# A hybrid HGRN2, pooling and gated MLP trunk: a new column pitch for the Strassen quarters, another order around the mixer's seam, and deferred sums in the down projection

## The chip, the core and the metric

The kernel runs on one core of one Trainium2 chip. The metric is the device time of one execution in microseconds, as the median of several runs. Profiles are of one execution, taken by the hardware profiler. The engines are TensorE (PE in the profile; its weight loads are PEld), VectorE (DVE), ScalarE (ACT), GpSimd (POOL) and SyncE (SP, which issues most of the DMAs).

## The reference

One layer over 16 meta tokens and 1024 tokens of width 1024, all in fp32:

```python
u = rmsnorm(h, mix_norm_pre)                     # h: meta tokens, then x
q, f_logit, i_in, g_out, v_pool, gate_a, gate_b = split(u @ w_in)
a = hgrn2(q, f_logit, i_in, g_out, lbs, hgrn_out_norm)     # chunked recurrence, 4 heads
p = multiscale_pool(v_pool, pool_proj, pool_scale)         # windows 2, 4, 8, 16
z = sigmoid(gate_a) * (a @ w_branch_hgrn) + sigmoid(gate_b) * (p @ w_branch_pool)
h = h + rmsnorm(z @ w_out, mix_norm_post)
u = rmsnorm(h, ffn_norm_pre)
gt = causal_dwconv(u @ ffn_w_gate, ffn_conv_w, ffn_conv_b) # 3 taps along the tokens
y = (gelu_tanh(gt) * (u @ ffn_w_up)) @ ffn_w_down          # inner width 2816
h = h + rmsnorm(y, ffn_norm_post)                          # meta tokens dropped
```

## The kernel before, in words

**fp32 by three matmuls.** Each operand is split into a rounded part (`h`, `hi`) and the rest (`l`, `lo`), and a product is the sum of hi by hi, hi by lo and lo by hi, accumulated in PSUM. ACT makes the rounded part by a cast, DVE (at places POOL) the rest by a subtraction. `wsplit2` (L159 and L160) does this for the weights of the branch projections, `keep` (L917 and L918) for weights of the feed-forward that are prepared early and stored in DRAM (`kept...`), `wo_split` (L1201) for the output projection, `cut` (L1494 and L1495) for the down projection.

**Strassen.** The gates of the mixer and the gate and up projections of the feed-forward run in units by Winograd's form of Strassen's scheme: the weights and the activations are cut into quarters, and a unit has seven products P1, P2, P6, P5, P3, P7, P4 in this order, whose moving operands are the quarters b11, b21 and b22 and the sums t1 to t4 (P1: b11, P2: b21, P6: t2, P5: t1, P3: b22, P7: t3, P4: t4). A quarter has four blocks of 128 rows (one column of a tile each, `k`) with the tokens along the free axis. The causal convolution needs two tokens of halo ahead of the first half of the tokens, so b11, b21, t2 and t4 have 514 columns: two of halo, then 512. A gate unit uses all 514, in two cuts of 258 and 256 columns, for P1, P2, P6 and P4; an up unit needs no halo and reads 512 columns from column 2 on. P5, P3 and P7 are 512 columns without a halo. In `product` (L299, L300 and L302) a block of 512 columns is three matmuls, a block with a halo six of half the size. In the mixer's gates b11, b21 and b22 are columns of the normed tokens themselves (`uhi` and `ulo`, rows of 1088 columns); in the feed-forward they are cut from one large tile, b11 and b21 from `v1` (rows of 544 columns, 514 used) and b22 and t1 from `v2` (rows of 512). t2 and t4 are made by `two_halves` in slots of their own (rows of 514), t1 of the mixer and t3 too (rows of 512). A row is 4 bytes per column.

**Order by hand.** Between the gates and the end of the mixer the string `ORDER` sets which work comes after which: F, Q, G and PV are input projections, h steps of the heads, BB and BA the eight column blocks of the two branch projections (pool and hgrn), `sa` splits of the heads' outputs, and w0 to w5 steps that prepare the feed-forward's weights (`keep_first` and `keep_unit`). The branch weights come in pairs that share one raw load, one cast and one subtraction: (BB6, BA2), then (BB7, BA3), (BA4, BA5), (BA6, BA7). They are asked for a few jobs ahead.

**The mixer's output projection** runs in three chunks c of 2, 3 and 3 tiles of 128 tokens (`TILES`), each with eight steps over the inner blocks; the last two steps run tile by tile. A tile's sums stand in a pair of PSUM banks (`pm`); there are four pairs. `Row` holds what follows, in steps that the table `SEAM` sets among the steps of the next chunk: `take` reads the pair twice (DVE: `m`, L1332; ACT: the square, `junk`, L1333), `add` scales it and adds the residual row, `square` and `norm` are the norm ahead of the feed-forward, `feat` transposes the row on PE into the quarters. A number is the tile, m the meta rows, W splits the next weights.

**Down projection.** It too is cut by Strassen-like sums, in three groups `s_` of 11 steps k, each with two sets of four banks, `pa` and `pb`, and 24 matmuls a step (L183 to L185); `prep` casts the operands for two steps ahead into two turns of one tile `rot`. At the end of a group the banks are joined into SBUF sums c11, c12, c21, c22 and u2 (`acc`). After group 1, u2 = pb - c11, c21 = pa - u2 and c12 = c12 - u2. DVE does the first two from PSUM (L1694, L1695), POOL the last (L1696). The order of the instructions of this part on each engine is found by the compiler's scheduler, unlike that of the mixer, which is as written.

Of the kernel before, what the change touches and what calls it, by code (L numbers as in the profile page):

```python
# [9 lines left out]
F32R = mybir.dt.float32r  # L10
U8 = mybir.dt.uint8
AF = mybir.ActivationFunctionType
ALU = mybir.AluOpType
# [7 lines left out]
HALO = 2  # L21
# [7 lines left out]
SEAM = (("W", "W", "W", "W", "W", "W", "0.take 0.add", "W 0.square 1.take m.join 0.norm 1.add 1.square 1.norm"),  # L29
# [14 lines left out]
HT = 514  # L44
HN = HT - HALO
EARLY = 4
# [11 lines left out]
         "w4 sa2 BB3 w5 h3 BB4 w5 BB5 w5 sa0 sa3 BA0 w5 BA1 w2 BB6 w3 BA2 BB7 BA3 BA4 BA5 BA6 BA7")  # L58
# [10 lines left out]
def trunk_kernel(ctx: ExitStack, tc: tile.TileContext, x, meta_tokens, mix_norm_pre,  # L69
# [897 lines left out]
    def two_halves(dst, q):  # L967
        n = HN if q in ("t1", "t3") else HT
        for h in "hl":
            dst[q + h] = [slot(2 * n, F32R, q + h).rearrange("p (k t) -> p k t", k=2) for _ in range(2)]  # L970
# [159 lines left out]
    gens, after = {}, {}  # L1130
# [43 lines left out]
    for n, name, names in ((HT, "v1", ("b11h", "b11l", "b21h", "b21l")), (HN, "v2", ("b22h", "b22l", "t1h", "t1l"))):  # L1174
        v = ubig(F32R, name)
        v1 = v if n == HT else v1
        t = v.rearrange("p (i k t) -> p i k t", i=4, k=4)
        for i, q in enumerate(names):
            fq[q] = [t[:, i, :, :n] if n == HT else t[:, i, :, :].rearrange("p k t -> p (k t)")[:, : 4 * n].rearrange("p (k t) -> p k t", k=4)]
# [70 lines left out]
    def to_quarters(un, t_at, n, pt, eng):  # L1250
# [6 lines left out]
        if t_at < HT:  # L1257
            src = pt.rearrange("p (j k t) -> p j k t", j=2, k=4) if n == P else pt.rearrange("p j (k t) -> p j k t", k=4)
            hi, lo = (v1.rearrange("p (j h k t) -> p h j k t", j=2, h=2, k=4)[:, h, :, :, t_at : t_at + n] for h in range(2))
            act.copy(hi, src)  # L1260
            dve.tensor_tensor(lo, src, rr(hi), ALU.subtract)
            return {}
# [258 lines left out]
    def step(c, at, after=None):  # L1521
        w = wo.next()
        for i in TILES[c]:
            mix_tile(c, at, w, R[i].x, i - TILES[c][0])
            if after:
                after(i)
        if c == 0:
            mix_meta(at, w, R["m"].x)
        wo.ahead()
        next_z(1)  # L1530
# [17 lines left out]
    with tc.manual_schedule(engines={E.PE, E.Activation, E.DVE, E.Pool}):  # L1548
        for i in (1, "m", 0):
            R[i] = Row(0 if i == "m" else HALO + i * P, HALO if i == "m" else P, pair("pm"))  # L1550
        for c in range(3):
            for at in range(KD - LAST):
                step(c, at)
                run(*SEAM[c][at].split())
# [116 lines left out]
    for s_ in range(3):  # L1671
        banks = [[bank("pd") for _ in range(NT)] for _ in range(2)]
        for k in range(KH):
            at = s_ * KH + k
            for b_, o_ in zip(banks, preps.pop(at)):
                multiply(b_, o_, k == 0, k == KH - 1)
            ahead(at + 2)
            if at >= 3 and early and at % 3 == 0:
                load_ops(3, early[0][0])
            if at >= 3 and early and at % 3 == 1:  # L1680
                prep_last(*early.pop(0))
            if s_ == 2 and k in (KH - 6, KH - 4):
                for t in ((0, 1) if k == KH - 6 else (2, 3)):
                    load_h(NT + t)
            if s_ == 2 and k == KH - 3:
                load_ops(3, KH - 2)
                load_ops(3, KH - 1)
        pa, pb = banks
        for t in range(NT):
# [3 lines left out]
            elif s_ == 1:  # L1693
                dve.tensor_tensor(u2[t], pb[t], c11[t], ALU.subtract)  # L1694
                dve.tensor_tensor(c21[t], pa[t], u2[t], ALU.subtract)  # L1695
                pool_e.tensor_tensor(c12[t], c12[t], u2[t], ALU.subtract)  # L1696
# [55 lines left out]
```

## Time and profile before

| what | value |
|---|---|
| median of 3 runs | 1349.35 us (1348.93 to 1350.22) |
| the profiled execution, its own time | 1351.27 us |
| its span in the profile | 1349.6 us |
| mean granted TensorE clock | 0.995 |
| 500 to 575 us | branch projections BB, BA: PE busy 74.33 of 75.00 us |
| 575 to 700 us | mixer's output projection: PE busy 124.22 of 125.00 us |
| 700 to 1120 us | feed-forward gate and up: PE busy 419.99 of 420.00 us |
| 1120 to 1290 us | its end and the down projection: PE busy 167.45 of 170.00 us |

A profile row names the engine, the line and the operation, what it writes and reads, shapes and counts. Times are microseconds unless marked ns. A timeline row begins with the start and the duration; in square brackets stand the idle time of the engine before it and what released it. A PE matmul's duration includes its way through the array: the next one starts before it ends. A row of the groups ends with busy time, mean ns of one, and idle time before.

### The profile page before, as it was taken

To read this page: it belongs to the slowest core of one execution; us is meant where nothing else is said; L and a number is where in the kernel's file an instruction comes from. 1 tells how busy PE (TensorE), PEld (TensorE's weight loads), DVE (VectorE), ACT (ScalarE), POOL (GpSimd) and SP (SyncE) were. 2 spreads that over 40 slices of the span, in tenths; PEclk is the share of its full clock that TensorE was granted. 3 is DMA by queue.
4 is the path that set the end of the run, shared out by engine and by line. 5 is a ranking of instruction groups with operands and counts; after the bars stand their busy time and mean duration, and the time that the engine had idled before them with its cause. 6 is when DMAs were issued, how large, how long until landed. Compare 5 with 4: busy or idle time off the path is not lost. (4 is left out here: it accounts for less than half of the span.)

```text
span 1349.6 us, 19941 instructions
## 1 busy us (share of the span) xinstructions
PE 1330.9 (99%) x7721; PEld 1184.0 (88%) x7721; DVE 975.9 (72%) x1232; ACT 561.8 (42%) x931; POOL 440.4 (33%) x331
## 2 busy tenths in 40 slices
PE   8999999999999999999999999999999999999997
PEld 6799999999999999987889888888888887888786
DVE  6755644389875857775768999888888886654557
ACT  6543333365464475224664322222222223543343
POOL 2014521236352610042015556546555642000100
PEclk9999999998999999999999999999999999999999
DMA  7134333311110139977586777776777799955624
GB/s 268 43 117 149 118 118 109 102 48 48 34 50 19 34 111 316 316 272 251 201 309 226 201 207 198 203 203 151 180 163 142 177 243 308 380 190 188 187 94 156
DMA packets 139665, 230.38 MB, mean 171 GB/s; under 512 B 9000, under 2 KB 77196, under 8 KB 139570
## 3 DMA queue, kind: packets, MB, share of 16 engines
q1 hardware_dynamic: 127506, 204.71, 44.7%
q0 software_dynamic: 12064, 24.38, 10.9%
q8 instruction: 61, 1.00, 0.3%
q14 instruction: 34, 0.28, 0.1%
HBM read 165.56 MB, written 86.53 MB: 187 GB/s over the span
## 5 line engine op out<-in xcount | busy, mean ns | idle before, releaser
L299 PE MATMUL P<-v,whi 128*128 128x512 f32 (+2 forms) x408 | 141.7, 355 | 0.0
L300 PE MATMUL P<-v,whi 128*128 128x512 f32 (+2 forms) x408 | 141.1, 353 | 0.0
L302 PE MATMUL P<-v,wlo 128*128 128x512 f32 (+2 forms) x424 | 136.0, 351 | 0.0
L184 PE MATMUL pd<-rot 128*128 128x512 f32 x272 | 106.0, 390 | 0.3 <-DVE rot L1495 0.3
L185 PE MATMUL pd<-rot 128*128 128x512 f32 x272 | 105.8, 389 | 0.0
L1495 DVE TENSOR_TENSOR rot<-yt,rot 128x1024 fp32r<-128x1024 f32 x33 | 41.2, 1249 | 71.3 <-ACT rot L1494 70.8
L300 PEld LDWEIGHTS P<-v,whi 128*128 128x128 f32 x408 | 77.2, 189 | 10.5
L299 PEld LDWEIGHTS P<-v,whi 128*128 128x128 f32 x408 | 77.2, 189 | 10.3
L270 POOL TENSOR_TENSOR swa<-wraw,wraw 128x512 f32<-128x512 f32 x28 | 40.9, 1462 | 134.2 <-DMA wraw<-in_ffn_w_gate_dram 70.4
L302 PEld LDWEIGHTS P<-v,wlo 128*128 128x128 f32 x424 | 74.3, 188 | 11.4
L244 ACT CAST whi<-wraw 128x512 fp32r<-128x512 f32 x78 | 46.1, 618 | 87.6 <-PE P L300 55.8
L183 PE MATMUL pd<-rot 128*128 128x512 f32 x272 | 72.8, 390 | 2.3 <-ACT rot L1494 2.2
L1494 ACT CAST rot<-yt 128x1024 fp32r<-128x1024 f32 x33 | 34.6, 1052 | 89.6 <-PE pd L184 89.6
L245 DVE TENSOR_TENSOR wlo<-swb,whi 128x512 fp32r<-128x512 f32 x56 | 62.7, 1126 | 6.7 <-ACT whi L244 6.6
L244 ACT CAST whi<-swa 128x512 fp32r<-128x512 f32 x56 | 33.4, 618 | 81.2 <-PE P L300 78.4
L1423 DVE SCALAR_TENSOR_TENSOR y<-g,par,y 128x1024 f32<-128x1024 f32 x44 | 64.6, 1467 | 0.8
L245 DVE TENSOR_TENSOR wlo<-wraw,whi 128x512 fp32r<-128x512 f32 x74 | 62.4, 865 | 1.4 <-ACT whi L244 1.4
L183 PEld LDWEIGHTS pd<-rot 128*128 128x128 f32 x272 | 50.9, 188 | 14.0 <-ACT rot L1494 3.0
L244 ACT CAST whi<-swb 128x512 fp32r<-128x512 f32 x56 | 33.4, 618 | 68.4 <-PE P L300 64.7
L184 PEld LDWEIGHTS pd<-rot 128*128 128x128 f32 x272 | 51.1, 188 | 11.3 <-DVE rot L1495 0.7
L185 PEld LDWEIGHTS pd<-rot 128*128 128x128 f32 x272 | 51.0, 188 | 10.6
L300 PE MATMUL P<-t4l,whi 128*128 128x258 f32 (+1 forms) x196 | 57.1, 308 | 0.0
(408 smaller groups left out, 4144.1 us busy)
## 6 DMA issues: line engine op xcount, KB each, us to landing
wraw<-in_w_in_dram SPq DMA_DIRECT2D x36, 512.0 KB, 4.3
yt<-ysum SPq DMA_DIRECT2D x33, 512.0 KB, 3.8
wraw<-in_ffn_w_gate_dram SPq DMA_DIRECT2D x26, 512.0 KB, 8.2
wraw<-in_ffn_w_up_dram SPq DMA_DIRECT2D x22, 512.0 KB, 5.7
wsum<-in_ffn_w_down_dram SPq DMA_DIRECT2D x22, 512.0 KB, 9.0
wraw<-in_w_out_dram SPq DMA_DIRECT2D x18, 512.0 KB, 4.4
ysum<-ys SPq DMA_DIRECT2D x11, 768.0 KB, 8.3
sa<-sscr SPq DMA_DIRECT2D x16, 513.0 KB, 6.1
```

The source lines that it names most:

```text
L183: pe.matmul(ps, ahi, bhi, start=first, stop=False)
L184: pe.matmul(ps, ahi, blo, start=False, stop=False)
L185: pe.matmul(ps, alo, bhi, start=False, stop=last)
L244: act.copy(hi, src)
L245: (pool_e if 4 <= i < 2 * self.early else dve).tensor_tensor(lo, src, rr(hi), ALU.subtract)
L270: pool_e.tensor_tensor(s1, a21, a22, ALU.add)
L299: pe.matmul(d, whi[:, k, :], xh[:, c : c + w], start=(k == 0 and onto is None), stop=False, **go)
L300: pe.matmul(d, whi[:, k, :], xl[:, c : c + w], start=False, stop=False, **go)
L302: pe.matmul(x[:, o : o + w], wlo[:, k, :], xh[:, c : c + w], start=False, stop=(k == 3), **go)
L1423: dve.scalar_tensor_tensor(a, g[:, j : j + SEQ], cvw[:, j, m : m + 1], a, ALU.mult, ALU.add)
L1494: act.copy(hi, src)
L1495: dve.tensor_tensor(lo, src, rr(hi), ALU.subtract)
```

## The change

- The quarters with a halo (b11, b21 of the feed-forward, t2 and t4 of both) get rows of 528 columns (`HP`), with the halo in columns 14 and 15 (`HO`) and the 512 columns behind it from column 16, which is byte 64. t1, t3 and b22 stay at rows of 512.
- In `ORDER`, "BA0 w5 BA1 w2 BB6 w3 BA2" becomes "BA0 BA1 w5 BB6 w2 BA2 w3".
- In `SEAM`, row 1's `take` moves ahead of row 0's `add` at the end of chunk 0; in chunk 1 row 0's `feat` comes ahead of the next cast of z (the new "|": what stands before it runs inside `step`), and the meta rows' `feat` one tile later.
- In the down projection c21 is at first only a copy of pa (on ACT). The subtractions of u2 from c21 and c12 are done by DVE in group 2, at steps 1 and 2. POOL has no part in it. The last operands are prepared at another remainder of three.

```diff
@@ -26,8 +26,8 @@
 KS = (range(8), range(7, -1, -1), range(8))
 LAST = 2
 LATE_ON_POOL = tuple(HALO + i * P for i in (4, 5, 6))
-SEAM = (("W", "W", "W", "W", "W", "W", "0.take 0.add", "W 0.square 1.take m.join 0.norm 1.add 1.square 1.norm"),
-        ("", "W 0.feat 1.load", "W 1.feat m.joined m.take", "W m.add m.square", "W m.norm", "W m.feat", "2.take 2.add", "2.square 3.take 2.norm 3.add", "W 3.square 4.take 3.norm 4.add 4.square 4.norm"),
+SEAM = (("W", "W", "W", "W", "W", "W", "0.take", "1.take 0.add W 0.square m.join 0.norm 1.add 1.square 1.norm"),
+        ("", "0.feat | W 1.load", "W 1.feat m.joined m.take", "W m.add m.square", "W m.norm", "W", "m.feat 2.take 2.add", "2.square 3.take 2.norm 3.add", "W 3.square 4.take 3.norm 4.add 4.square 4.norm"),
         ("2.load", "W 2.feat", "W", "3.feat W quarters", "4.feat W 4.sums 4.t2 4.neg", "W 4.t1 4.b22",
          "5.take 4.d3 5.add 4.t3", "5.square 6.take 5.norm 6.add 4.t4", ""))
 SEAM4 = ("6.square 5.feat 7.take 6.norm 7.add", "7.square 5.sums 7.norm", "6.feat 5.t2 5.neg 6.sums", "", "7.feat 6.t2 6.neg 7.sums", "7.t2 5.t1 6.t1", "", "7.neg 7.t1 5.b22", "6.b22 5.d3 6.d3 7.b22", "5.t3 7.d3 6.t3 7.t3 5.t4 6.t4 7.t4")
@@ -43,6 +43,8 @@
 KT = 6
 HT = 514
 HN = HT - HALO
+HP = 528
+HO = 16 - HALO
 EARLY = 4
 EARLY_G = 2
 SUMS_AT = {5: (2,), 6: (2, 1), 8: (3,), 9: (1, 3), 10: (1, 4), 11: (4, 0), 12: (0, 0)}
@@ -55,7 +57,7 @@
 
 ORDER = ("F0 c0 Q0 h0 F1 h0 c1 Q1 h0 h1 F2 h1 c2 h0 Q2 h1 h2 G2 h0 h1 h2 h0 F3 h0 h2 c3 PV0 h1 h2 h1 Q3 h3 h1 h3 h1 "
          "PV1 h3 sp0 PV2 h2 h3 sa1 sp1 sp2 PP0 h2 PV3 h2 h3 sp3 PP1 h0 G3 w0 h3 PP2 h3 PP3 w1 BB0 w4 h2 BB1 w4 BB2 "
-         "w4 sa2 BB3 w5 h3 BB4 w5 BB5 w5 sa0 sa3 BA0 w5 BA1 w2 BB6 w3 BA2 BB7 BA3 BA4 BA5 BA6 BA7")
+         "w4 sa2 BB3 w5 h3 BB4 w5 BB5 w5 sa0 sa3 BA0 BA1 w5 BB6 w2 BA2 w3 BB7 BA3 BA4 BA5 BA6 BA7")
 POOLED = ("e1k.0 e1k.3 kdmul.2 kdmul.3 kdsub.2 lk32.1 lk4.1 lk64.0 lq16.1 lq16.3 lq32.0 lq32.1 lq32.2 lq4.0 "
           "lq64.0 lq64.3 lq8.0 lq8.1 lq8.2 osg.2 qsmul.2 qsmul.3 sub2.2 sub32.1 sub4.1 sub8.1 sub8.3 wBA2 wBA6 "
           "wBA7 wBB2 wF0 wF2 wF3 wPP2 wPV0 wPV1 wPV2 wPV3 wQ0 wQ1 wQ3").split()
@@ -965,9 +967,10 @@
             gq[q + h] = [u[:, 4 * i : 4 * i + 4, t0 : t0 + n]]
 
     def two_halves(dst, q):
-        n = HN if q in ("t1", "t3") else HT
+        n, o = (HN, 0) if q in ("t1", "t3") else (HP, HO)
         for h in "hl":
-            dst[q + h] = [slot(2 * n, F32R, q + h).rearrange("p (k t) -> p k t", k=2) for _ in range(2)]
+            dst[q + h] = [slot(2 * n, F32R, q + h).rearrange("p (k t) -> p k t", k=2)[:, :, o : o + (HT if o else HN)]
+                          for _ in range(2)]
 
     def halo_sums(bq, d):
 
@@ -1171,12 +1174,11 @@
 
 
     fq, v1 = {}, None
-    for n, name, names in ((HT, "v1", ("b11h", "b11l", "b21h", "b21l")), (HN, "v2", ("b22h", "b22l", "t1h", "t1l"))):
-        v = ubig(F32R, name)
-        v1 = v if n == HT else v1
-        t = v.rearrange("p (i k t) -> p i k t", i=4, k=4)
-        for i, q in enumerate(names):
-            fq[q] = [t[:, i, :, :n] if n == HT else t[:, i, :, :].rearrange("p k t -> p (k t)")[:, : 4 * n].rearrange("p (k t) -> p k t", k=4)]
+    for name, names in (("v1", ("b11h", "b11l", "b21h", "b21l")), ("v2", ("b22h", "b22l", "t1h", "t1l"))):
+        n, o = (HP, HO) if name == "v1" else (HN, 0)
+        t = ubig(F32R, name)[:, : 16 * n].rearrange("p (i k t) -> p i k t", i=4, k=4)
+        v1 = v1 or t
+        fq.update({q: [t[:, i, :, o : o + (HT if o else HN)]] for i, q in enumerate(names)})
 
     def add_quarters(*names):
         for q in names:
@@ -1256,7 +1258,7 @@
         pt = pt[:, : 8 * n] if n == P else pt.rearrange("p (j t) -> p j t", j=2)[:, :, : 4 * n]
         if t_at < HT:
             src = pt.rearrange("p (j k t) -> p j k t", j=2, k=4) if n == P else pt.rearrange("p j (k t) -> p j k t", k=4)
-            hi, lo = (v1.rearrange("p (j h k t) -> p h j k t", j=2, h=2, k=4)[:, h, :, :, t_at : t_at + n] for h in range(2))
+            hi, lo = (v1.rearrange("p (j h) k t -> p h j k t", h=2)[:, h, :, :, HO + t_at : HO + t_at + n] for h in range(2))
             act.copy(hi, src)
             dve.tensor_tensor(lo, src, rr(hi), ALU.subtract)
             return {}
@@ -1518,12 +1520,11 @@
         for i in TILES[c]:
             R[i] = Row(HALO + i * P, P, pair("pm"))
 
-    def step(c, at, after=None):
+    def step(c, at, *first):
         w = wo.next()
         for i in TILES[c]:
             mix_tile(c, at, w, R[i].x, i - TILES[c][0])
-            if after:
-                after(i)
+        run(*first)
         if c == 0:
             mix_meta(at, w, R["m"].x)
         wo.ahead()
@@ -1550,8 +1551,9 @@
             R[i] = Row(0 if i == "m" else HALO + i * P, HALO if i == "m" else P, pair("pm"))
         for c in range(3):
             for at in range(KD - LAST):
-                step(c, at)
-                run(*SEAM[c][at].split())
+                first_, _, then_ = SEAM[c][at].rpartition("|")
+                step(c, at, *first_.split())
+                run(*then_.split())
             if c == 2:
                 ffn.ahead(2)
             ws = []
@@ -1675,9 +1677,13 @@
             for b_, o_ in zip(banks, preps.pop(at)):
                 multiply(b_, o_, k == 0, k == KH - 1)
             ahead(at + 2)
+            if s_ == 2 and k in (1, 2):
+                for t in range(NT):
+                    c = (c21, c12)[k - 1][t]
+                    dve.tensor_tensor(c, c, u2[t], ALU.subtract)
             if at >= 3 and early and at % 3 == 0:
                 load_ops(3, early[0][0])
-            if at >= 3 and early and at % 3 == 1:
+            if at >= 3 and early and at % 3 == 2:
                 prep_last(*early.pop(0))
             if s_ == 2 and k in (KH - 6, KH - 4):
                 for t in ((0, 1) if k == KH - 6 else (2, 3)):
@@ -1691,9 +1697,8 @@
                 act.copy(c11[t], pa[t])
                 dve.tensor_copy(c12[t], pb[t])
             elif s_ == 1:
+                act.copy(c21[t], pa[t])
                 dve.tensor_tensor(u2[t], pb[t], c11[t], ALU.subtract)
-                dve.tensor_tensor(c21[t], pa[t], u2[t], ALU.subtract)
-                pool_e.tensor_tensor(c12[t], c12[t], u2[t], ALU.subtract)
             else:
                 dve.scalar_tensor_tensor(c22[t], c12[t], -1.0, pa[t], ALU.mult, ALU.subtract)
                 dve.tensor_tensor(c21[t], c21[t], pa[t], ALU.add)
```

The engines' rows at three places. First ACT, in the branch projections, before; `whi_5203` is the cast of the weights of BB6 and BA2, `whi_5329` that of BB7 and BA3, the L917 rows are w5 (those from `wlo_5217` and `wraw_5084`), w2 and w3:

```order
L159 CAST whi_5203<-wraw_5202 128x1024
L917 CAST whi_5216<-wlo_5217 128x512 x2
L917 CAST whi_5283<-wraw_5084 128x512
L159 CAST whi_5329<-wraw_5328 128x1024
L917 CAST whi_5343<-wraw_5341 128x512 x2
L917 CAST whi_5398<-wraw_5396 128x512 x2
```

And now, where `whi_5325` is the cast for BB7 and BA3, and `whi_5434` that for BA4 and BA5:

```order
L161 CAST whi_5203<-wraw_5202 128x1024
L919 CAST whi_5216<-wlo_5217 128x512 x2
L161 CAST whi_5325<-wraw_5324 128x1024
L919 CAST whi_5335<-wraw_5084 128x512
L919 CAST whi_5387<-wraw_5385 128x512 x2
L161 CAST whi_5434<-wraw_5433 128x1024
L919 CAST whi_5450<-wraw_5448 128x512 x2
```

The cast for BB7 and BA3 has moved ahead of the second cast of w5, and the one for BA4 and BA5 ahead of that of w3.

Second ACT at the end of chunk 0, before; `pm_5824` is the pair of banks of row 0 and `pm_5822` that of row 1:

```order
L1333 ACTIVATE junk_833_6005,ssq_831_6004<-pm_5824 128x1024
L1337 ACT_TABLE_LOAD
L1337 ACTIVATE std_6008<-ssq_831_6004,eps_t 128x1
L1352 ACTIVATE un_6038,ssq_6037<-m_830_6003 128x1024
L1337 ACTIVATE std_6040<-ssq_6037,eps_t 128x1
L1333 ACTIVATE junk_845_6044,ssq_843_6043<-pm_5822 128x1024
L1321 COPY pmh_6047<-pm_5823 4x1024
```

And now:

```order
L1335 ACTIVATE junk_833_6005,ssq_831_6004<-pm_5824 128x1024
L1335 ACTIVATE junk_840_6033,ssq_838_6032<-pm_5822 128x1024
L1339 ACT_TABLE_LOAD
L1339 ACTIVATE std_6036<-ssq_831_6004,eps_t 128x1
L1354 ACTIVATE un_6043,ssq_6042<-m_830_6003 128x1024
L1339 ACTIVATE std_6045<-ssq_6042,eps_t 128x1
L1323 COPY pmh_6047<-pm_5823 4x1024
```

The read of row 1's pair now follows at once on that of row 0's, ahead of row 0's root and square.

Third, DVE in the down projection at the turn from group 1 to group 2, before; `pd_10969` to `pd_10972` are the banks pa, `pd_10973` to `pd_10976` pb, and the rot rows the operands of steps 1 and 2 of group 2:

```order
L1694 TENSOR_TENSOR acc_10511<-pd_10973,acc_10511 128x512
L1694 TENSOR_TENSOR acc_10511<-pd_10974,acc_10511 128x512
L1695 TENSOR_TENSOR acc_10511<-pd_10969,acc_10511 128x512
L1694 TENSOR_TENSOR acc_10511<-pd_10975,acc_10511 128x512
L1694 TENSOR_TENSOR acc_10511<-pd_10976,acc_10511 128x512
L1695 TENSOR_TENSOR acc_10511<-pd_10970,acc_10511 128x512
L1495 TENSOR_TENSOR rot_10512<-yt_11275,rot_10512 128x1024
L1695 TENSOR_TENSOR acc_10511<-pd_10971,acc_10511 128x512
L1495 TENSOR_TENSOR rot_10512<-wraw_11276,rot_10512 128x1024
L1695 TENSOR_TENSOR acc_10511<-pd_10972,acc_10511 128x512
L1495 TENSOR_TENSOR rot_10512<-yt_11312,rot_10512 128x1024
```

And now, where `pd_10969` to `pd_10972` are pb, and L1683 are the deferred subtractions:

```order
L1701 TENSOR_TENSOR acc_10511<-pd_10969,acc_10511 128x512
L1701 TENSOR_TENSOR acc_10511<-pd_10970,acc_10511 128x512
L1683 TENSOR_TENSOR acc_10511<-acc_10511 128x512 x2
L1701 TENSOR_TENSOR acc_10511<-pd_10971,acc_10511 128x512
L1701 TENSOR_TENSOR acc_10511<-pd_10972,acc_10511 128x512
L1683 TENSOR_TENSOR acc_10511<-acc_10511 128x512 x2
L1497 TENSOR_TENSOR rot_10512<-yt_11275,rot_10512 128x1024
L1497 TENSOR_TENSOR rot_10512<-wraw_11276,rot_10512 128x1024
L1683 TENSOR_TENSOR acc_10511<-acc_10511 128x512 x4
L1497 TENSOR_TENSOR rot_10512<-yt_11308,rot_10512 128x1024
```

Only four rows read PSUM; the subtractions that were between the two rot rows of step 1 stand ahead of them or behind. PE's order at the same place, before, from the 25th matmul of group 2 on; `pd_11369` to `pd_11372` are pa and `pd_11373` to `pd_11376` pb:

```order
L183 MATMUL pd_11375<-rot_10512 128x512
L184 MATMUL pd_11375<-rot_10512 128x512
L185 MATMUL pd_11375<-rot_10512 128x512
L183 MATMUL pd_11375<-rot_10512 128x512
L184 MATMUL pd_11369<-rot_10512 128x512
L185 MATMUL pd_11369<-rot_10512 128x512
L184 MATMUL pd_11370<-rot_10512 128x512
L185 MATMUL pd_11370<-rot_10512 128x512
L184 MATMUL pd_11371<-rot_10512 128x512
```

And now, with `pd_11365` to `pd_11368` as pa and `pd_11369` to `pd_11372` as pb:

```order
L185 MATMUL pd_11371<-rot_10512 128x512
L186 MATMUL pd_11371<-rot_10512 128x512
L187 MATMUL pd_11371<-rot_10512 128x512
L185 MATMUL pd_11371<-rot_10512 128x512
L185 MATMUL pd_11372<-rot_10512 128x512
L186 MATMUL pd_11372<-rot_10512 128x512
L187 MATMUL pd_11372<-rot_10512 128x512
L185 MATMUL pd_11372<-rot_10512 128x512
L186 MATMUL pd_11365<-rot_10512 128x512
```

The first matmuls on the last bank of pb follow directly on those of the third; before, its first row is the 43rd of group 2, 14 rows later.

## The prediction

> **What bounds the kernel now.** The page comes first, for the shares of the engines:
>
> ```profile
> span 1349.6 us, 19941 instructions
> PE 1330.9 (99%) x7721; PEld 1184.0 (88%) x7721; DVE 975.9 (72%) x1232; ACT 561.8 (42%) x931; POOL 440.4 (33%) x331
> ```
>
> TensorE (PE) is busy in 99% of the span, and no engine beside it and its own weight loads is over 72%. So only two things move the time: how soon one matmul may start after another, and the gaps in PE's stream. The gaps are in the table of what PE waited for (total us, times, longest). These are the rows whose places the change edits:
>
> ```profile
> PE pd L183 <- ACT rot L1494: 2.2, 2, 1.2
> ...
> PE pm L183 <- ACT junk L1333: 0.8, 1, 0.8
> ...
> PE pbb L196 <- ACT whi L159: 0.3, 1, 0.3
> PE pbb L200 <- DVE wlo L160: 0.3, 1, 0.3
> PE pd L184 <- DVE rot L1495: 0.3, 1, 0.3
> ```
>
> Together they are 2.9 us, counting of the first row only its longest wait, the one in the edited place. The table is too low, though: it counts idle time, and a matmul counts as busy until its modelled end, long after the next could have started. So from here on I take differences of start times from the timeline; what a stall costs is the difference less the step of an undisturbed stream. The forecast is a sum of four terms: one speed and three gaps.
>
> **Part 1, the rows at a pitch of 528.** A product of the Strassen scheme with 512 columns is 12 matmuls (4 blocks of 128 rows, 3 matmuls each). In PE's timeline, these are the first matmuls of consecutive products, first P7 (t3) and P4 (t4) of one up unit and P1 of the next gate unit, and then P1, P6 (t2) and P5 (t1, under the name v) of an up unit and the product after:
>
> ```profile
> 1084.75 0.39 PE L299 MATMUL P<-t3h,whi 128*128 128x512 f32 x1
> ...
> 1087.47 0.40 PE L299 MATMUL P<-t4h,whi 128*128 128x512 f32 x1
> ...
> 1090.26 0.28 PE L299 MATMUL P<-v,whi 128*128 128x258 f32 x1
> ...
> 1109.94 0.39 PE L299 MATMUL P<-v,whi 128*128 128x512 f32 x1
> ...
> 1115.58 0.40 PE L299 MATMUL P<-t2h,whi 128*128 128x512 f32 x1
> ...
> 1118.37 0.40 PE L299 MATMUL P<-v,whi 128*128 128x512 f32 x1
> ...
> 1121.14 0.39 PE L299 MATMUL P<-v,whi 128*128 128x512 f32 x1
> ```
>
> P7 takes 2.72 us, which is 0.227 per matmul; P4 takes 2.79. P1 and P2 take 5.64 together, 2.82 each; P6 takes 2.79 and P5 2.77. What separates them in the code is the place of the rows: t3's 512 columns start at column 0 of rows of 2048 bytes, while those of P1, P2, P6 and P4 start two columns (8 bytes) into rows of 2176 or 2056 bytes. P5's rows lie as t3's do, yet it follows P6 and is 0.05 slow; I read that as an after-effect of the product ahead of it. If the slowness comes from the 8 bytes, an up unit gains 0.10 on P1, 0.10 on P2, 0.07 on P6, 0.05 on P5 and 0.07 on P4: 0.39 us. How many such units there are, and how many of the edited products carry the halo, is in the groups kept apart by shape:
>
> ```profile
> L300 PE MATMUL P<-t2l,whi 128*128 128x512 f32 x44 | 17.5, 397 | 0.0
> L300 PE MATMUL P<-t2l,whi 128*128 128x258 f32 x76 | 21.5, 283 | 0.0
> L300 PE MATMUL P<-v,whi 128*128 128x258 f32 x72 | 20.4, 283 | 0.0
> ```
>
> Of this line a product has 4 matmuls of a shape, so there are 11 P6 without a halo (44 by 4), one for each up unit: 11 x 0.39 = 4.3 us. With a halo, in two cuts of 258 and 256 columns, there are 19 P6 (76 by 4), as many P4, and 18 P1 and P2 of the feed-forward (72 by 4). Their new place is already seen once: the mixer's gates read P1 and P2 from uhi, whose columns start 256 bytes into rows of 4352.
>
> ```profile
> 168.40 0.28 PE L299 MATMUL P<-uhi,whi 128*128 128x258 f32 x1
> ...
> 174.07 0.28 PE L299 MATMUL P<-t2h,whi 128*128 128x258 f32 x1
> ...
> 1096.03 0.28 PE L299 MATMUL P<-t2h,whi 128*128 128x258 f32 x1
> ...
> 1098.90 0.39 PE L299 MATMUL P<-v,whi 128*128 128x512 f32 x1
> ```
>
> There P1 and P2 take 5.67 together, 2.84 each; in the feed-forward they take 5.77 (1090.26 to 1096.03) and P6 2.87. So the halo products gain at most 9 x 0.10 + 38 x 0.035 = 2.2 us, and perhaps nothing. I take nothing, since of so small a difference one pair of products is thin proof, and keep 2.2 for the range. Term 1 is 4.3, between 0 and 6.5. What ACT and DVE write into these rows is the same in number and size, so nothing is added there.
>
> A rule speaks against this term. The Trainium skill, on the page "SBUF — State Buffer", section "Specifications (TRN2)", says that SBUF has lines of 16 bytes and that each crossing to a new line costs something. By it a row of 512 fp32 values that is shifted by 8 bytes touches 129 lines where an aligned one touches 128: an estimate from that page of under 1% of a matmul, and a term 1 of some 0.9 us. By the rows the shift goes with 8 ns of a matmul's 227 (2.82 against 2.72 us over 12 matmuls), 3.7%, so the rule alone doesn't explain them.
>
> **Part 2, BA1 before w5.** PE, ACT and DVE where the product BB7 begins:
>
> ```profile
> 559.03 1.05 ACT L159 CAST whi<-wraw 128x1024 fp32r<-128x1024 f32 x1 [4.81 <-issue]
> 559.15 0.63 PE L200 MATMUL pba<-ah,wlo 128*128 128x342 f32 x3
> ...
> 560.12 0.44 PE L196 MATMUL pbb<-phi,whi 128*128 128x342 f32 x1 [0.34 <-ACT whi L159]
> 560.40 1.23 DVE L160 TENSOR_TENSOR wlo<-wraw,whi 128x1024 fp32r<-128x1024 f32 x1 [2.92 <-DMA kept8l<-wlo]
> ...
> 561.04 0.32 PE L197 MATMUL pbb<-plo,whi 128*128 128x342 f32 x1
> ...
> 561.68 0.42 PE L200 MATMUL pbb<-phi,wlo 128*128 128x342 f32 x1 [0.33 <-DVE wlo L160]
> ```
>
> Matmuls of 342 columns are 0.16 apart (three of them in the row at 559.15 end 0.63 later, the last having its own latency of 0.32). So BB7 would have started at 559.63 and started at 560.12: 0.49 lost; the second wait costs 561.68 - 561.04 - 0.16 = 0.48. The first matmul after each takes 0.44 and 0.42 where its neighbour takes 0.32, another 0.1 each, so 1.0 to 1.2; I take 1.1. The weights' cast comes at 559.03 after 4.81 us of idle ACT. In the new order it stands ahead of w5's second cast and takes over that one's turn at a whi buffer, by the time that ACT went idle: 559.03 - 4.81 = 554.2. DVE's half is moved up in the same way. DVE was idle from 560.40 - 2.92 = 557.5, so even behind all that it did before, its pass of 1.23 ends by 558.7, 0.9 ahead of 559.63; what ends last there is then PE's own BA2. What is moved the other way: w5's second pair with its two stores on SP's queue, and behind them on that queue the load for w3. w3's tiles are read back only in the feed-forward, and the weights of BA4 and BA5 are now asked for ahead of them. The term is 1.1, between 0 (another late buffer) and 1.2.
>
> **Part 3, the seam between mixer chunks 0 and 1.** A chunk is a third of the rows; its last sums leave PSUM by `take`, one read on DVE and one on ACT, and only then may the third tile of the next chunk use that pair of banks.
>
> ```profile
> 625.61 1.06 ACT L1352 ACTIVATE un<-m 128x1024 f32<-128x1024 f32 x1 [1.55 <-DVE m L1347]
> ...
> 626.98 0.39 PE L185 MATMUL pm<-whi,zc 128*128 128x512 f32 x1
> 627.00 1.00 ACT L1333 ACTIVATE junk<-pm 128x1024 f32<-128x1024 f32 x1
> ...
> 628.14 0.50 PE L183 MATMUL pm<-whi,zc 128*128 128x512 f32 x1 [0.78 <-ACT junk L1333]
> 628.48 0.40 PE L184 MATMUL pm<-wlo,zc 128*128 128x512 f32 x1
> ```
>
> PE loses 628.14 - 626.98 - 0.23 = 0.93, and 0.34 - 0.23 = 0.11 on the next step: 1.04. Row 1's read on ACT stands behind row 0's square root and square (625.61), which wait for DVE. With 1.take ahead of 0.add, the read is the next thing on ACT after row 0's own. ACT was idle for 1.55 ahead of 625.61, so it has the time for it by 624.1 at the latest, 2.9 us before 627.00, and the wait of 0.93 is gone. In return row 0's add, square and norm slip by one DVE pass and one ACT pass, 2 to 3 us, and with it its store on SP's queue, which nobody reads before the end. Row 0's transposes (0.feat) come several tiles of PE work later; that is what hides the slip. If it isn't enough, PE waits there instead, at most by about what is won here. The term is 1.0, between 0 and 1.04.
>
> **Part 4, the down projection.** PE, DVE and ACT at the start of the third group of sums (s_ = 2):
>
> ```profile
> 1255.78 1.71 DVE L1495 TENSOR_TENSOR rot<-wraw,rot 128x1024 fp32r<-128x1024 f32 x1
> ...
> 1256.86 0.39 PE L183 MATMUL pd<-rot 128*128 128x512 f32 x1
> 1257.41 0.68 DVE L1695 TENSOR_TENSOR acc<-pd,acc 128x512 f32<-128x512 f32 x1
> ...
> 1257.54 0.50 PE L184 MATMUL pd<-rot 128*128 128x512 f32 x1 [0.29 <-DVE rot L1495]
> 1257.88 0.39 PE L185 MATMUL pd<-rot 128*128 128x512 f32 x1
> ...
> 1261.50 1.05 ACT L1494 CAST rot<-yt 128x1024 fp32r<-128x1024 f32 x1 [8.79 <-PE pd L184]
> ...
> 1261.98 0.39 PE L185 MATMUL pd<-rot 128*128 128x512 f32 x1
> ...
> 1263.55 0.74 PE L183 MATMUL pd<-rot 128*128 128x512 f32 x2 [1.18 <-ACT rot L1494]
> ```
>
> First gap: 0.68 - 0.23 + 0.34 - 0.23 = 0.56. Second: 1263.55 - 1261.98 - 0.23 = 1.34, with the slow step behind it 1.45. Together 2.0. The second has its cause in the order of PE: the last bank of step k = 0 is freed only by DVE's subtraction of c21 (the row at 1257.41 is the last of them), so its matmuls were put at the end of k = 1, and the rot buffer that they read is not cast again for k = 2 before 1261.50. Now pa leaves PSUM by four copies on ACT (at most 1.05 each, the cast of twice the columns), which fit into its 8.79 us of idle time, DVE has only four sums that read PSUM, and the last bank comes 14 matmuls sooner, 14 x 0.227 = 3.2 us: more than the 1.34. DVE's work is larger by the four sums that POOL had, 4 x 0.68 = 2.7 at most, spread over two steps. Each step has 24 matmuls, 24 x 0.227 = 5.4 us of PE, in which DVE must fit two rot passes (1.71 at the worst) and four sums, 6.1 with these worst rows; so DVE is the unknown of this term. The sums stand ahead of both rot passes of k = 1 or behind them, no longer between them, and POOL has none of its own at that time. The term is 2.0, between 0 (DVE late in its turn) and 2.0. That the last operands are prepared at another remainder of three moves no row of ACT, DVE or PE: nothing.
>
> **The sum.** 4.3 + 1.1 + 1.0 + 2.0 = 8.4 us. The profiled execution took 1351.27, its span of 1349.6 and 1.67 around it, 1.92 above the median of 1349.35; nothing in the four places depends on that difference, so the saving is set against the median: 1341.0.
>
> **The rivals.** *The 8 bytes aren't the cause.* For it: P5, whose rows lie well, is at 2.77 too. Against: t4 is slow at once behind t3, which is not. Then term 1 is 0 and the time 1349.35 - 4.1 = 1345.3. A milder form: the shift costs only the extra memory that a row touches, at most 4 columns' worth of 512, which is 44 products x 2.8 us x 4/512 = 1.0, and 1344.3. The rule of the skill's SBUF page, above, would have it so.
>
> *A stall moves instead of going.* Either DVE's sums hold up rot, or row 0's transposes wait. Against it are the idle times above; for it, that DVE's sum of worst rows is 6.1 in 5.4. One of them kept costs 1.0 to 2.0: 1342.0 to 1343.0.
>
> *The new pitch is worse than the old.* This one ends slower. 528 columns are 2112 bytes, an odd multiple of 64; the clean rows of this trace lie 2048 or 4352 apart, and none shows such a spacing. It would act on 44 full products (11 x P1, P2, P6, P4) and 56 with a halo, 12 full-length matmuls or their worth each: 1200. At another 8 ns each that is +9.6 - 4.1, 1354.9. It decides from (4.1 + 2.7) / 1200 = 5.7 ns. Against it: P1, at 2176 bytes, and t4, at 2056, differ by only 0.03 us a product, so spacing seems to matter little.
>
> **How the numbers follow.** A measurement of this kernel can tell about 0.2%, 2.7 us, from no change. Forecast 0.58, rival one 0.16, rival two 0.14, rival three 0.12, of which 0.03 falls within 0.2%. All but the third are faster by over 2.7 us: faster 0.88, same 0.03, slower 0.09. The forecast's own range is 1339.0 (2.0 of the halos' 2.2 gained as well) to 1342. Rivals one and two reach to 1345.3; with 0.3 for the measurement the range is 1339.0 to 1345.6, which leaves out the third and the tails.
>
> **What would show it.** Right: products P1, P2, P6 and P4 of the up units at 2.72 to 2.74 us, the group t2l 128x512 near 389 ns instead of 397; the rows pbb, pm and pd L184 gone from PE's waits, and pd L183 down to 1.0. Wrong: t2l still at 397 (rival one), a new wait of pt for un or of pd L184 for rot (rival two), t2l over 397 or the 258-column groups over 283 (rival three).

## The result and the profile after

The kernel after takes 1344.83 us (median of 8 runs, 1341.38 to 1347.15) against 1349.78 for the kernel before in the same runs: a ratio of 0.9959, interval 0.9947 to 0.9971, which is 3.9 to 7.2 us faster. A second set of 6 runs gave 0.9951 (0.9938 to 0.9963). The forecast was 1341.0 in a range of 1339.0 to 1345.6.

The profiled execution took 1347.15, its span is 1345.4, 4.2 less than before. First the page, then what PE waited for (total us, times, longest):

```profile
span 1345.4 us, 19942 instructions
...
PE 1328.6 (99%) x7721; PEld 1183.5 (88%) x7721; DVE 972.1 (72%) x1236; ACT 563.7 (42%) x935; POOL 438.1 (33%) x327
```

```profile
PE pba L198 <- DVE sa L872: 1.8, 3, 1.3
...
PE pd L185 <- ACT rot L1496: 0.8, 1, 0.8
...
PE P L301 <- ACT sg L801: 0.7, 1, 0.7
...
PE pm L185 <- DVE sa L872: 0.4, 1, 0.4
```

The rows pbb, pm for junk and pd for DVE's rot are gone, and pd for ACT's rot is down from 2.2 to 0.8. A row is new that no step of the prediction had at that place: PE waits three times for DVE's reads of the banks pba, 1.8 us, and once for the same at the mixer's start. The wait for ACT's sg, in the first 110 us, was 0.2 before; it is 0.7 in every trace with the new rows and 0.2 in those without, and why was not followed.

To see what each stage gained, take the starts of the first matmul of the branch projections, of the mixer, of the feed-forward and of the down projection, in PE's timeline of the kernel before and then of the kernel after:

```profile
498.31 0.40 PE L196 MATMUL pbb<-phi,whi 128*128 128x342 f32 x1
...
595.13 0.40 PE L183 MATMUL pm<-whi,zc 128*128 128x512 f32 x1
...
696.24 0.28 PE L299 MATMUL P<-v,wraw 128*128 128x258 f32 x1
...
1129.37 0.40 PE L183 MATMUL pd<-rot 128*128 128x512 f32 x1
```

```profile
497.96 0.40 PE L198 MATMUL pbb<-phi,whi 128*128 128x342 f32 x1
...
596.54 0.47 PE L185 MATMUL pm<-whi,zc 128*128 128x512 f32 x1 [0.35 <-DVE sa L872]
...
696.53 0.28 PE L301 MATMUL P<-v,wraw 128*128 128x258 f32 x1
...
1127.27 0.39 PE L185 MATMUL pd<-rot 128*128 128x512 f32 x1
```

| stretch | before | after | difference | forecast |
|---|---|---|---|---|
| up to the branch projections | 498.3 | 498.0 | -0.3 | 0 |
| branch projections | 96.8 | 98.6 | +1.8 | -1.1 |
| mixer's output projection | 101.1 | 100.0 | -1.1 | -1.0 |
| feed-forward, gate and up | 433.1 | 430.7 | -2.4 | -4.3 |
| down projection, to the end | 220.2 | 218.1 | -2.1 | -2.0 |

Two of the four terms came out to about a tenth of a microsecond. The rows brought about half of their term, and the new order of BA1 and w5 has the other sign in this execution.

**The rows.** These are the first matmuls of P4 of an up unit, of P1 of the gate unit behind it, of its P6 (t2) and P5, and then of P1, P6, P5 and P3 of the next up unit, in PE's timeline after:

```profile
1085.55 0.40 PE L301 MATMUL P<-t4h,whi 128*128 128x512 f32 x1
...
1088.36 0.28 PE L301 MATMUL P<-v,whi 128*128 128x258 f32 x1
...
1094.05 0.28 PE L301 MATMUL P<-t2h,whi 128*128 128x258 f32 x1
...
1096.89 0.39 PE L301 MATMUL P<-v,whi 128*128 128x512 f32 x1
...
1107.92 0.39 PE L301 MATMUL P<-v,whi 128*128 128x512 f32 x1
...
1113.48 0.40 PE L301 MATMUL P<-t2h,whi 128*128 128x512 f32 x1
...
1116.28 0.39 PE L301 MATMUL P<-v,whi 128*128 128x512 f32 x1
...
1119.03 0.39 PE L301 MATMUL P<-v,whi 128*128 128x512 f32 x1
```

P1 and P2 take 5.56 us, 2.78 each, where 2.72 was forecast and 2.82 was before. P6 at 2.80 and P4 at 2.81 are a little slower than the 2.79 of before. P5 went from 2.77 to 2.75. The group of t2l without a halo is still where it was, at 397 ns before:

```profile
L302 PE MATMUL P<-t2l,whi 128*128 128x512 f32 x44 | 17.5, 398 | 0.0
```

That is the sign that the prediction gave for its rival one, that the 8 bytes aren't the cause. The products with a halo, valued at nothing, gained: P1 and P2 from 5.77 to 5.69, P6 from 2.87 to 2.84.

**The branch projections.** PE, ACT and DVE in BA3, where the longest new wait is:

```profile
561.69 0.62 ACT L919 CAST whi<-wraw 128x512 fp32r<-128x512 f32 x1 [4.95 <-issue]
...
565.67 1.14 ACT L919 CAST whi<-wraw 128x512 fp32r<-128x512 f32 x2 [3.36 <-DMA kept9l<-wlo]
...
565.88 0.32 PE L199 MATMUL pba<-al,whi 128*128 128x342 f32 x1
...
566.32 0.69 DVE L920 TENSOR_TENSOR wraw<-wraw,whi 128x512 fp32r<-128x512 f32 x1 [3.19 <-ACT whi L919]
...
566.93 1.35 DVE L872 TENSOR_TENSOR sa<-sa,pba 128x342 f32<-128x342 f32 x3
...
567.49 0.42 PE L198 MATMUL pba<-ah,whi 128*128 128x342 f32 x1 [1.28 <-DVE sa L872]
```

Read it from the bottom. PE needs the banks that BA2 filled (1.28). DVE empties them only from 566.93 on, since a subtraction of w2 stands ahead of that read in its queue. The subtraction waits for w2's cast at 565.67, and the cast waits for a store of w5's last tile, which was cast at 561.69. By its address in the built program w2's `whi` tile lies in the buffer of that w5 tile, so the store in its way is kept9h, the one that reads that buffer; the profile names kept9l, which was issued right behind it.

### The profile page after: what moved, and what is told of

It is laid out like the page before. It is cut to its first block, busy times and chain, and to the rows that moved or that the text cites. A ratio compares the mean times of both kernels' runs of the same rounds, so it can differ in the third digit from the quotient of the medians.

```text
span 1345.4 us, 19942 instructions
## 1 busy us (share of the span) xinstructions
PE 1328.6 (99%) x7721; PEld 1183.5 (88%) x7721; DVE 972.1 (72%) x1236; ACT 563.7 (42%) x935; POOL 438.1 (33%) x327
## 4 chain that ended last, share of the span: by engine, by line
PE 86%; DVE 6%; DMA 4%; issue 2%; ACT 2%; SPq 0%; DVEq 0%; ACTq 0%
PE P L301 15%; PE P L302 14%; PE P L304 14%; PE pd L185 5%; PE pd L186 5%; PE pd L187 5%; PE pm L185 2%; PE pm L187 2%; PE pm L186 2%; PE sl L668 2%; PE pq L198 1%; PE pv L186 1%; PE pq L202 1%; PE pq L199 1%; PE pv L187 1%
## 5 line engine op out<-in xcount | busy, mean ns | idle before, releaser
L301 PE MATMUL P<-t4h,whi 128*128 128x258 f32 (+1 forms) x196 | 57.0, 307 | 0.0
```

The costliest lines, as they stand in the source:

```text
L301: pe.matmul(d, whi[:, k, :], xh[:, c : c + w], start=(k == 0 and onto is None), stop=False, **go)
```

## The experiments

All ratios are of times, to the kernel before in the same runs. The stretches are worked out as in the table above.

### The four parts alone

Each is the kernel before with one part of the diff. The rows:

```diff
+HP = 528
+HO = 16 - HALO
```

> The kernel before with the new rows alone. Theory A (the trace after, read product by product): the rows are worth about 3.0 us; P1 and P2 of an up unit take 2.78 us instead of 2.82, halo products win a little, and P6 and P4 of an up unit stay at 2.79 to 2.81. Rival (the prediction): 4.3 us, all four at 2.72.

0.9980 (0.9967 to 0.9993): 0.9 to 4.5 us faster. The feed-forward takes 430.7 us against 433.1: 2.4, as in the kernel after. Theory A's 3.0 was a little high, the forecast's 4.3 far too high.

```diff
-BA0 w5 BA1 w2 BB6 w3 BA2
+BA0 BA1 w5 BB6 w2 BA2 w3
```

> The kernel before with the new order of BA1 and w5 alone. Theory A: it costs 1.5 to 2.5 us; the waits of pbb (1.2 us by start times) go, and PE waits instead for DVE's reads of the pba banks (about 1.3 at one place, some 0.3 at two or three others), since those reads stand behind a subtraction of w2 that waits for a cast. Rival (the prediction): it saves 1.1, and the new waits in the trace after come from the other parts.

0.9995 (0.9981 to 1.0008): no difference that the runs can tell. The branch projections take 96.1 us, 0.7 under before. PE's waits:

```profile
PE pba L196 <- DVE sa L870: 0.3, 1, 0.3
```

That is all that came in place of both pbb rows. So theory A, which read a cost of 1.5 to 2.5 out of one trace, fell for this execution, and so did the full 1.1.

```diff
-"0.take 0.add", "W 0.square 1.take m.join 0.norm 1.add 1.square 1.norm"
+"0.take", "1.take 0.add W 0.square m.join 0.norm 1.add 1.square 1.norm"
```

> The kernel before with the new table of the seam alone. Theory A: it saves 1.0 us; the wait of pm for the read of row 1's pair is gone and no wait of a transpose takes its place. Rival: row 0's slip makes the transposes wait and the sum is 0 to 0.5.

0.9991 (0.9979 to 1.0002). The mixer's stretch is 99.9 us against 101.1, the row pm for junk is gone and no wait of pt for the mixer's rows is new. The slip of row 0 is hidden, as the prediction had it.

```diff
+                act.copy(c21[t], pa[t])
                 dve.tensor_tensor(u2[t], pb[t], c11[t], ALU.subtract)
-                dve.tensor_tensor(c21[t], pa[t], u2[t], ALU.subtract)
-                pool_e.tensor_tensor(c12[t], c12[t], u2[t], ALU.subtract)
```

> The kernel before with the deferred sums of the down projection alone. Theory A: it saves 2.0 us, both gaps at the start of group 2 are gone. Rival: DVE is late with rot, and only the first gap goes: 0.6.

0.9983 (0.9970 to 0.9995): 0.7 to 4.0 us faster. The last stretch is 217.8 us against 220.2. Both gaps at the start of group 2 are gone, and DVE is in time: in the kernel after, its last rot pass of step 1, four of the deferred sums and its first rot pass of step 2 stand as follows, with ACT's cast for step 2:

```profile
1253.49 1.22 DVE L1497 TENSOR_TENSOR rot<-wraw,rot 128x1024 fp32r<-128x1024 f32 x1
...
1254.63 2.49 DVE L1683 TENSOR_TENSOR acc<-acc 128x512 f32<-128x512 f32 x4
...
1255.71 1.06 ACT L1496 CAST rot<-yt 128x1024 fp32r<-128x1024 f32 x1 [5.02 <-PE pd L186]
...
1257.04 1.22 DVE L1497 TENSOR_TENSOR rot<-yt,rot 128x1024 fp32r<-128x1024 f32 x1
```

The pass that took 1.71 takes 1.22, the four sums 2.49 together, and DVE turns to rot right after its four sums.

### The order once more

The kernel after again, and without its new order:

> The kernel after, unchanged, once more. Theory A: its waits of pba for DVE's reads (3.1 us by start times in the first trace of it) are built into its order and come again, 2 us or more. Theory B: they depend on when the stores of the prepared weights land in the one execution, since with the new order alone they were 0.6; then they are under 1.2 here.

> The kernel after with the old order of BA1 and w5. Theory A: 1 to 2 us faster than the kernel after. Theory B: 0.5 to 1 us slower, with the waits of pbb back (1.0 to 2.4 us by start times).

Both are at 0.9951 (0.9938 to 0.9963, and 0.9938 to 0.9965). So in company with the other parts the new order is worth nothing that these runs can see; neither theory has its sign. The second trace of the kernel after has 98.5 us in the branch projections, the kernel with the old order 97.2. PE's waits in the first:

```profile
PE pm L185 <- DVE sa L872: 1.2, 1, 1.2
PE pba L198 <- DVE sa L872: 1.0, 2, 0.7
```

The same two waits as in the first trace, of another size, and 0.3 with the new order alone. Theory A's part that holds is the kind of wait; theory B's is that its size depends on the execution.

To see whether DVE's queue is the cause, w2 goes behind BA2 and w3 behind BA3:

```diff
-BA0 BA1 w5 BB6 w2 BA2 w3 BB7 BA3 BA4
+BA0 BA1 w5 BB6 BA2 w2 BB7 BA3 w3 BA4
```

> The kernel after with w2 behind BA2 and w3 behind BA3 (BA0 BA1 w5 BB6 BA2 w2 BB7 BA3 w3). Theory A (in the kernel after, DVE's reads of BA2's banks stand behind a subtraction of w2, which waits for a store): with them ahead of it the wait inside BA3 goes, the stretch from the first BB matmul to the first of the mixer is 96.0 us or less, against 98.5 in the kernel after and 97.1 with the old order, and the time is 1 to 2 us under the kernel after. Rival: the next reads wait instead, and the stretch stays over 97.

0.9952 (0.9936 to 0.9967). The waits of pba are gone, and the stretch is 96.7 us, under both the 98.5 and the 97.2, though not at theory A's 96.0. One wait stays, at the mixer's start:

```profile
PE pm L185 <- DVE sa L872: 0.8, 1, 0.8
```

It has another cause. DVE and POOL there:

```profile
591.52 2.81 DVE L1124 TENSOR_TENSOR zc<-sa,zc 128x256 fp32r<-128x256 f32 x1
591.61 2.42 POOL L1205 TENSOR_TENSOR wlo<-wraw,whi 128x1024 fp32r<-128x1024 f32 x1
...
594.32 1.34 DVE L872 TENSOR_TENSOR sa<-sa,pba 128x342 f32<-128x342 f32 x3
...
595.39 0.47 PE L185 MATMUL pm<-whi,zc 128*128 128x512 f32 x1 [0.77 <-DVE sa L872]
```

A subtraction on DVE that took 0.42 elsewhere in the branch projections takes 2.81 while POOL works on 1024 columns for 2.42, and the read of PSUM behind it comes late by as much. The Trainium skill, "SBUF — State Buffer", section "Terms", says of the port pair that DVE and GpSimd share that the loser "fully blocks". The two rows agree in that DVE ends 0.3 after POOL; which of the two came first they don't tell, as DVE's row begins 0.09 ahead of POOL's.

So the traces show that the wait inside BA3 came from w2's place in DVE's queue. The gain of 1 to 2 us on the whole time that theory A gave is not shown, as the interval is 4 us wide.

### The place of the rows

All four are the kernel with the old order (e6_no_order) with other rows. In the built programs the tiles that the quarters are cut from begin on multiples of 256 bytes, so where a row starts within 256 bytes follows from the start and the pitch alone. First rows of 544 columns, the 512 columns from byte 128, so that every second row starts 128 bytes into a stretch of 256 and the others on a multiple of it:

```diff
-HP = 528
-HO = 16 - HALO
+HP = 544
+HO = 32 - HALO
```

> The kernel of e6_no_order with rows of 544 columns for all quarters with a halo and the 512 columns behind it from column 32: byte 128, and each second row on a multiple of 256. Theory C (a multiple of 128 bytes is enough): P1, P2, P6 and P4 of an up unit at 2.72 us, 2.5 to 3 us faster than e6_no_order. Theory D (it takes 256): they stay near 2.77 to 2.80 and the time within 1 us of e6_no_order.

0.9968 (0.9956 to 0.9980), the feed-forward at 430.9 us against 430.8: no gain over 64 bytes. P6 and the product behind it start as follows:

```profile
1113.25 0.39 PE L301 MATMUL P<-t2h,whi 128*128 128x512 f32 x1
...
1116.03 0.40 PE L301 MATMUL P<-v,whi 128*128 128x512 f32 x1
```

P6 takes 2.78. Theory C fell. Theory D holds for the products but not for its time, within 1 us of e6_no_order: the median is 2.3 us over it. No stage of the two traces shows a loss of that size; the granted clock was 0.995 to 0.998 in these runs and 0.996 to 0.999 in those of e6_no_order.

The seven later up units read b22 and t3 instead, on rows of 2048 bytes. They leave out b11, b21, t2 and t4, so the output is no longer that of the layer:

```diff
+            if c0 == HALO and u >= 2 * EARLY:
+                q, c0 = dict(P1="b22", P2="b22", P6="t3", P4="t3")[p], 0
```

> The kernel of e6_no_order in which the seven later up units read b22 in place of b11 and b21, and t3 in place of t2 and t4: the same matmuls and weights, on rows of 2048 bytes from column 0. Their results are left wrong. Theory C or D (the place of the rows is the cause): these products take 2.72 us, and the time is 7 x 0.3 = 2.1 us under e6_no_order. Rival: the cause lies in the products (weights, banks, neighbours), they stay at 2.78 to 2.80 and nothing is gained.

Of the groups by shape, this is the one that now holds the seven units' P6 and P4 too (before: 120 matmuls, 389 ns), and then what is left on t2:

```profile
L303 PE MATMUL P<-t3h,whi 128*128 128x512 f32 x176 | 68.5, 389 | 0.0
...
L304 PE MATMUL P<-t2l,whi 128*128 128x512 f32 x16 | 6.4, 397 | 0.0
```

The same weights on other rows run at 389 ns. So the place of the rows is the cause, not the product. In time nothing came of it (0.9975, 0.9961 to 0.9989): the feed-forward is 1.0 us shorter than with the rows of 528, not 2.1, since PE now stalls at the start of two products of the last up unit and the gate units in between lose some 0.04 each, and PE waits longer early in the down projection:

```profile
PE pd L185 <- ACT rot L1498: 2.6, 1, 2.6
```

b11 and b21 in rows of 576 columns, from byte 256, so that every row starts on a multiple of 256:

```diff
-        n, o = (HP, HO) if name == "v1" else (HN, 0)
+        n, o = (576, 64 - HALO) if name == "v1" else (HN, 0)
-FM_SLOTS = 26
+FM_SLOTS = 25
```

> The kernel of e6_no_order with b11 and b21 in rows of 576 columns and their 512 columns from column 64, so that each starts on a multiple of 256 bytes; one slot fewer for it to fit. t2 and t4 stay at 528. Theory D (rows on multiples of 256 stream at full rate): P1 and P2 of an up unit at 2.72 us, the feed-forward 1.0 to 1.5 us shorter than the 430.75 of e6_no_order. Rival (only rows of 2048 bytes do): P1 and P2 stay at 2.78, the stretch at 430.5 to 431.

P1 of an up unit, its P6, and P5:

```profile
1104.86 0.39 PE L301 MATMUL P<-v,whi 128*128 128x512 f32 x1
...
1110.30 0.40 PE L301 MATMUL P<-t2h,whi 128*128 128x512 f32 x1
...
1113.11 0.39 PE L301 MATMUL P<-v,whi 128*128 128x512 f32 x1
```

P1 and P2 take 5.44, 2.72 each: theory D holds, at full rate. P6, left at 528, stays at 2.81. The feed-forward is at 430.3 us, 0.5 shorter than at 528 where 1.0 was expected at least, since products with a halo lose part of it again: P1 and P2 of a gate unit take 2.87 and 2.88 where both took 2.85, and P6, whose rows were not moved, 2.86 in place of 2.84. Why is not shown. The whole kernel is at 0.9963 (0.9950 to 0.9976), no faster than e6_no_order at 0.9951.

Last, rows of 528 with the halo at column 0 and the 512 columns from byte 8:

```diff
-HO = 16 - HALO
+HO = 0
```

> The kernel of e6_no_order with the rows at 528 columns but the halo at column 0 again, the 512 columns from byte 8. Theory (the start on a multiple of 64 bytes is what helped): the feed-forward is back at 433.1 us, P1 and P2 at 2.82. Rival (the pitch helped, not the start): it stays at 430.8.

0.9985 (0.9975 to 0.9995) where e6_no_order has 0.9951. The feed-forward is back at 433.1 us. P1 and P2 of an up unit, from P1 to P6:

```profile
1106.83 0.39 PE L301 MATMUL P<-v,whi 128*128 128x512 f32 x1
...
1112.44 0.39 PE L301 MATMUL P<-t2h,whi 128*128 128x512 f32 x1
```

5.61, 2.81 each against 2.82 before, and as P6 and P4 are a little slower than before (2.82 and 2.83), the unit as a whole takes what it took. The new pitch alone does nothing; with the same pitch, the start does. No run has a pitch that is a multiple of 256 bytes and a start that is not.

### Both that helped

The order of e9_order2 and the rows of e10_v1_576 together:

> Both changes that helped together, on the kernel after: the order of e9_order2 and the rows of e10_v1_576 (the feed-forward's b11 and b21 on multiples of 256 bytes). If they add up, the stretch of the branch projections is 96.7 us or less and the feed-forward 430.3, and the time about 0.5 us under e9_order2, 6 to 8 us under the kernel before. Rival: with one slot fewer a wait comes back and the two don't add up.

1343.0 us, 0.9949 (0.9932 to 0.9966). The branch projections take 96.4 us, the feed-forward 430.3, the mixer 100.0 and the last stretch 217.8: the gains of the traces add up. In time it beats the kernel before by 4.6 to 9.2 us, but the runs can't tell it from the kernel after (0.9951 and 0.9959).

## Why the prediction was right, and where it was not

**The bound** was right: PE's share is 99% in both traces, and the time changed by what its stream lost or gained.

**Part 1** had the right cause and the wrong size. The step that failed is "0.10 on P1, 0.10 on P2, 0.07 on P6, 0.05 on P5 and 0.07 on P4": it took a start on byte 64 for as good as t3's start on byte 0. P1 and P2 gained 0.04 each and P5 0.02, P6 and P4 lost 0.01 each; in place of 0.39 a unit that is some 0.07, 0.8 us over 11 units. The rest of the 2.4 us came from where I had put nothing: 0.08 on P1 and P2 of each of 9 gate units (0.7), 0.03 on a P6 with a halo, and the first products behind them. The bounds, 0 to 6.5, held it. What was missing is shown by two runs: on multiples of 256 bytes P1 and P2 take 2.72 us (e10_v1_576); where the rows start on multiples of 128 and only every second one on a multiple of 256, they stay slow (e7_row544). P5 as an after-effect of the product ahead of it was read rightly: behind a P6 on clean rows it takes 2.72 (e8_clean). The rival on the pitch is out: with the pitch alone (e11_col2) the feed-forward takes the same 433.1 us as before. The rival that the 8 bytes aren't the cause is out too, by e8_clean and e11_col2, although its sign came (t2l at 398 ns): t2 went from one slow place to another. By the lines of 16 bytes of which the Trainium skill tells ("SBUF — State Buffer", section "Specifications (TRN2)") the gain would have been an estimated 0.9 us in the place of 2.4, and rows on multiples of 64 and 128 would have been as good as those on 256. The traces show neither, so here the measurement decides.

**Part 2** failed in the sentence "w3's tiles are read back only in the feed-forward": that w5, w2 and w3 are not needed soon is true of their data, not of their places in DVE's queue. The new order string puts w2 ahead of BA2, so w2's subtraction (566.32 above) stands ahead of the reads of BA2's banks (566.93), and w2's cast now waits for a store that itself starts later: the two stores of w5's last tile are issued at 562.3 and 563.2, against 554.2 and 556.3 before. In place of 1.1 won, the stretch lost 1.8 in the first trace. The stall on pbb went as forecast; in both traces of the kernel after new waits took its place, and with w2 behind BA2 (e9_order2) those inside the branch projections went.

**Parts 3 and 4** were right in mechanism and size: 1.1 for 1.0 and 2.1 for 2.0, each also alone, with the waits gone from the rows and nothing late next. That part 4 came so close is in part luck: the last stretch also holds PE's first wait for ACT's rot, some 20 us into it, which no edit touched and which was 1.0 before and 0.8 after. Without it the stretch goes from 219.2 to 217.3, by 1.9. DVE, the unknown of part 4, needed 2.49 us for four sums beside an idle POOL, less than the 2.7 of the bound.

**The sum.** 2.4 + 1.1 + 2.1 and 0.3 ahead of the branch projections, less 1.8, is 4.1, against 4.2 between the two spans. The forecast's 8.4 lies outside the measured 3.9 to 7.2; that the range held the time is luck, since it reached so far for rivals one and two, and neither is what happened: it was half of term 1 and the sign of term 2. A stall did move, but neither to rot nor to the transposes, which are the places that rival two names.

**What stays open.** How much the new order is worth in company. The stretch has 98.6 and 98.5 us in its two traces there and 96.1 alone; with the old order it has 96.8 to 98.1 in nine traces (the wait of pbb for ACT is 0.3 to 1.4 in them), and the times of e5_again and e6_no_order are the same. Which stores land late in which execution was not followed further.

## What to carry to other kernels

When an operation is moved, read the queue of every engine it uses from the moved place on, and ask of each waiting instruction what stands behind it: a subtraction that nobody needs soon can still hold back the read that frees a PSUM bank. When one layout runs clean and another slow, don't assume which property of the clean one matters; name its whole alignment (t3's rows start on multiples of 256) before pricing a step towards it. And a gain read in one stage is safe only to the next wait for a DMA: look at what that wait will swallow.

## What the runs showed of the hardware

A stream of 512-column fp32 matmuls ran at 0.227 us each where all rows of the moving operand started on multiples of 256 bytes, and at 0.230 to 0.236 on average where some or all of them started 8 to 200 bytes into such a stretch. The wait for ACT's cast early in the down projection, behind a load, was between nothing and 1.8 us in the traces, and 2.6 in e8_clean, with no order by kernel.

The granted clock goes with most of the spread between runs of one kernel: the kernel after has spans of 1339.7 to 1341.2 us in its three runs at 0.998 and 0.999, and of 1342.9 to 1345.4 in its five at 0.995 to 0.997. The two profiles of the kernel after (the second is that of e5_again) differ by 4.2 us in span, and 4.0 of it lies ahead of the branch projections. The stretch from 300 to 320 us in the first and in the second (the columns: busy time and count of PE, PEld, DVE, ACT and POOL, then the granted clock, the share and rate of DMA):

```profile
300.00:320.00 20.00, 19.05 (x148) 18.49 (x148) 20.00 (x19) 12.68 (x22) 15.98 (x8) 0.87 0.19 53
```

```profile
300.00:320.00 20.00, 19.05 (x168) 18.50 (x168) 20.00 (x19) 12.69 (x22) 15.98 (x8) 1.00 0.19 54
```

In the same 20 us 148 matmuls were issued in the one and 168 in the other, and behind it the same matmul starts 3.0 us later in the first. The profile of the kernel before has 148 there too, at 0.88, so it and the first profile of the kernel after compare fairly. The clock is why a part that is worth 1 us is read from the stage's start times here and not from the time of the whole.
